# Attention scores of both maps in one double PSUM bank: one maximum for two, the output copy on ScalarE, two factor steps on GpSimd

## The chip, the core and the metric

The kernel runs on one core of one Trainium2 chip. The metric is device time in microseconds (us) of one execution. Of the engines, PE is the matrix engine (its weight loads are listed apart, as PEld), DVE is VectorE, ACT is ScalarE, POOL is GpSimd and SP issues transfers. Every engine works through its own list of instructions in order, and waits where an operand isn't ready.

## What is computed

One inference step of a decoder trunk of two layers, for a prompt of 2048 positions and 8 samples. The change lies in one part of the even layer, the differential attention of the prompt:

```python
def diff_core(q, k, v, allowed, lam):
    s = jnp.einsum('bqhcd,bkhcd->bhcqk', q, k).astype(jnp.float32) * (DIFF_DH ** -0.5)
    p = jax.nn.softmax(jnp.where(allowed, s, -jnp.inf), axis=-1)
    attn = p[:, :, 0] - lam * p[:, :, 1]
    return jnp.einsum('bhqk,bkhd->bqhd', attn.astype(v.dtype), v)
```

Each of 6 heads has two score maps (c = 0 and 1) of 64 channels each. Each map has its own softmax over the keys up to the query's position, and the values (128 wide) are weighted with the first map minus lam times the second. A block of 128 queries sees one to sixteen blocks of 128 keys. What follows per query is an RMS norm of the output.

## The kernel before

The program runs in stages: `in_even` (the input projection, up to about 788 us), `attention` (about 788 to 1395 us), `out_even` (to about 1700 us) and `odd` (the second layer). Only `attention` and the functions it calls are changed.

`attention` (L726) walks over 6 heads and in each over 16 query blocks i of 128 rows, ascending, in the last head descending. `attn_tile` (L789) does one query block. Its keys come in chunks of 512 (`nch` of them, 1 to 4; the last one is 128, 256, 384 or 512 wide).

- Per chunk and map, PE makes the scores `sc` with two matmuls, over the high and the low half of the split keys (L808, L809), and on the last chunk adds the causal mask with a third (L811). DVE takes the negated row maximum `nb` (L812), and ACT the exponential into `p` with the row sum in `l` (L813; the sum is read out by an instruction of its own, READ_ACCUMULATOR).
- When all chunks of the block have their maxima, the factor steps follow (L822 to L832): `m`, the maximum over the chunks (DVE, L824); `f = m - nb` (DVE, L825); exp of it (ACT, L826); `l*f` (DVE, L828), its sum `r` (L829), the reciprocal (L830), times -lam for the second map (L831), and `f*r` (L832), which leaves the factors in `cf`. Blocks with one chunk have two short steps instead (L819, L820).
- Per chunk, POOL multiplies the second map by its factor (L836); in three turns of four DVE then multiplies the first map and adds (L839, one instruction with two inputs), in the fourth POOL does that with two instructions (L841, L842). PE transposes the result, 128 columns at a time (L846, into `tr`), ACT copies it out of PSUM (L848), and PE multiplies it with the values into `pv` (L850).
- At the end of a block DVE copies `pv` to `ob` (L851), and ACT takes the sum of squares of the same `pv` (L853). After four blocks ACT and POOL normalise (L772, L773), PE transposes (`ot`, L783) and ACT scales (L785).

There are 240 chunks (168 of them 512 wide, 24 each of 384, 256 and 128), so 480 score tiles, and 96 blocks, 72 of them with two chunks or more.

PSUM has eight banks of 512 numbers per partition. `bank` (L79) hands them out by kind in turn, and `AT` names them for this stage: four single banks for `sc` ("XXDA", where X has two buffers), two for `tr`, one each for `pv` and `ot`. A bank is given to the next score tile when the exponential over the old one is done. The pool of banks is opened once for the whole program. There are 9 buffers for `p` (`PB`).

The order of the instructions on each engine is set when the program is built: by the order in which the code asks for them and by when the building program takes their inputs to be ready. Work of different chunks and blocks is so interleaved on each engine.

Of the kernel before, what the change touches and what calls it, by code (L numbers as in the profile page):

```python
# [10 lines left out]
F32 = mybir.dt.float32  # L11
# [9 lines left out]
P = 128  # L21
# [24 lines left out]
SP = 0  # L46
AT = dict(sc="XXDA", tr="Y", pv="B", ot="C")
W1, W2, WA, WB, WC = "P", "D", "P", "PD", "PD"
# [13 lines left out]
class Net:  # L62
    def __init__(self, tc, I, O, stop=99):
        self.tc, self.nc, self.I, self.O, self.stop = tc, tc.nc, I, O, stop
        self.root = ExitStack()
        self.const = self.pool(self.root, "const", 1)
        self.sides, self.pace, self.nturn = {}, PC, 0
        self.dram = self.pool(self.root, "dram", 1, DRAM)
        self.ps, self.nbank = self.pool(self.root, "ps", 1, PSUM), {}

    def pool(self, st, name, bufs, space=None, side=None):
# [3 lines left out]
        if side is not None:  # L75
            kw["side"] = side
        return st.enter_context(self.tc.tile_pool(name=name, bufs=bufs, **kw))

    def bank(self, kind, *shape):  # L79
# [617 lines left out]
    def lam_const(self):  # L697
# [13 lines left out]
        nc.vector.scalar_tensor_tensor(self.nlam, e[:, 1:2], -LAM0, e[:, 0:1], ALU.add, ALU.subtract)  # L711
        tmp.close()
        self.sub_w = c.tile([P, 1], F32, name="subw")
        nc.sync.dma_start(self.sub_w, I["subln_w"].rearrange("a d -> d a"), allow_slow_non_contiguous=True)
# [11 lines left out]
    def attention(self):  # L726
        st = ExitStack()
        nc, I = self.nc, self.I
        self.banks = AT


# [43 lines left out]
        self.attn_out(*done, sm)  # L775
        st.close()

    def attn_out(self, h, quad, ob, sm):
# [10 lines left out]
    def attn_tile(self, i, kvt, qt, o, oss, pp, tp, sm):  # L789
# [8 lines left out]
        with self.tc.high_priority(SP) if SP else nullcontext():  # L798
            for j in range(nch):
                n = min(512, nk * P - 512 * j)  # L800
                w = max(n, 256)
                kh, kl = kvt[j][:2]
                p = pp.tile([P, 2, 512], F32, tag="p", name="p")
                for c in range(2):
                    sc = self.bank("sc", 512)
                    qc = qt[:, c, q0:q0 + P]
                    last = j == nch - 1
                    mm(sc[:, :w], qc, kh[:, c, :w], start=True, stop=False)  # L808
                    mm(sc[:, :w], qc, kl[:, c, :w], start=False, stop=not last)  # L809
                    if last:  # L810
                        mm(sc[:, n - P:n], self.identb, self.maskb, start=False, stop=True)  # L811
                    nc.vector.tensor_reduce(nb[:, c, j:j + 1], sc[:, :n], AX.X, ALU.max, negate=True)  # L812
                    nc.scalar.activation(p[:, c, :n], sc[:, :n], AF.Exp, bias=nb[:, c, j:j + 1],  # L813
                                         accum_out=l[:, c, j:j + 1])
# [6 lines left out]
        else:  # L821
            r = sm.tile([P, 2], F32, tag="r", name="r")  # L822
            m = sm.tile([P, 2], F32, tag="m", name="m")
            nc.vector.tensor_reduce(m, nb[:, :, :nch], AX.X, ALU.min)  # L824
            nc.vector.tensor_tensor(f, m[:, :, None].broadcast_to([P, 2, nch]), nb[:, :, :nch], ALU.subtract)  # L825
            nc.scalar.activation(f, f, AF.Exp)  # L826
            lf = l[:, :, :nch]
            nc.vector.tensor_tensor(lf, lf, f, ALU.mult)  # L828
            nc.vector.tensor_reduce(r, lf, AX.X, ALU.add)  # L829
            nc.vector.reciprocal(r, r)  # L830
            nc.vector.tensor_scalar(r[:, 1:2], r[:, 1:2], self.nlam, None, ALU.mult)  # L831
            nc.vector.tensor_tensor(f, f, r[:, :, None].broadcast_to([P, 2, nch]), ALU.mult)  # L832
        pv = self.bank("pv", P)
        for j in range(nch):
# [14 lines left out]
            for t in range(nt):  # L849
                mm(pv, tt[:, t, :], kvt[j][2][:, t, :], start=j == 0 and t == 0, stop=j * 4 + t == nk - 1)  # L850
        nc.vector.tensor_copy(o, pv)  # L851
        junk = sm.tile([P, P], F32, tag="junk", name="junk", bufs=2)
# [800 lines left out]
    def run(self):  # L1653
# [10 lines left out]
        if self.stop > 3:  # L1664
            self.odd()
        self.oddst.close()
        self.root.close()

# [91 lines left out]
```

## Time and profile before

| | us |
|---|---|
| median of 3 runs | 3147.14 (3144.58 to 3152.71) |
| profiled execution, its own time | 3144.06 |
| span of that execution, first to last instruction | 3142.4 |

| stage, window | length | PE busy | PEld | DVE | ACT | POOL |
|---|---|---|---|---|---|---|
| input projection, 0 to 785 | 785 | 725.8 | 707.2 | 421.8 | 366.0 | 415.3 |
| attention, 785 to 1397 | 612 | 549.3 | 454.2 | 557.9 | 476.2 | 422.9 |
| output, 1397 to 1700 | 303 | 265.6 | 233.3 | 206.0 | 80.4 | 181.9 |
| second layer, 1700 to the end | 1443 | 1271.7 | 1121.2 | 984.4 | 593.7 | 668.3 |

Busy time is the union of an engine's instructions. Those of one engine overlap a little at their ends, and PE's a good deal: its matmuls are pipelined, so the distance from one start to the next is shorter than the duration shown. A row of a group gives busy time, mean duration, then the engine's idle time just before these instructions and what ended most of it.

### The profile page before, as it was taken

The numbers are of one execution on the slowest core, as the hardware profiler recorded it, in microseconds if no ns is written. First come the engines' busy times: TensorE is split into PE (matmuls) and PEld (weight loads), VectorE is DVE, ScalarE is ACT, GpSimd is POOL, SyncE is SP. The second block draws the span as 40 slices with busy tenths as digits, with TensorE's granted clock in tenths as the row PEclk, the third lists the DMA queues.
The fourth block names the chain that finished last, engine by engine and source line by source line (L and its number), as shares of the span: only waits on it lengthen the run. The fifth ranks groups of instructions, "written<-read, shape, count | busy, mean of one in ns | idle before, by whom it ended". The sixth has DMA issues, their size and how long they took to land. (4 is left out here: it accounts for less than half of the span.)

```text
span 3142.4 us, 57680 instructions
## 1 busy us (share of the span) xinstructions
PE 2812.4 (89%) x20425; PEld 2515.9 (80%) x20425; DVE 2170.1 (69%) x4012; ACT 1516.3 (48%) x4464; POOL 1688.4 (54%) x1220
## 2 busy tenths in 40 slices
PE   8999899989998899989888778999899988878999
PEld 7999799889777777778777667888788877767887
DVE  5465456464998899876669998658788575457562
ACT  6643245534877787752222223445554533344331
POOL 4566545571667776664665655455544244255541
PEclk9999899999999999999998889999999999979999
DMA  4567766556244423237765554435333233467543
GB/s 164 167 192 254 240 219 202 190 166 183 70 102 118 121 60 84 71 101 221 245 217 180 164 164 160 130 103 154 86 95 100 82 99 112 121 159 212 164 119 98
DMA packets 423149, 462.55 MB, mean 147 GB/s; under 512 B 84683, under 2 KB 324212, under 8 KB 422860
## 3 DMA queue, kind: packets, MB, share of 16 engines
q1 hardware_dynamic: 422860, 458.86, 49.5%
q8 instruction: 162, 2.65, 0.4%
q14 instruction: 127, 1.04, 0.1%
HBM read 332.41 MB, written 126.33 MB: 146 GB/s over the span
## 5 line engine op out<-in xcount | busy, mean ns | idle before, releaser
L184 PE MATMUL acc<-sh,whi 128*128 128x256 f32 (+2 forms) x1328 | 392.5, 296 | 7.4 <-ACT raw L1211 4.8
L186 PE MATMUL acc<-sh,wlo 128*128 128x256 f32 (+2 forms) x1328 | 389.6, 294 | 1.5 <-DVE wlo L165 1.2
L185 PE MATMUL acc<-sl,whi 128*128 128x256 f32 (+2 forms) x1328 | 389.6, 293 | 0.0
L184 PE MATMUL acc<-bh,whi 128*128 128x512 f32 (+2 forms) x904 | 347.4, 384 | 23.9 <-ACT raw L1211 11.2
L186 PE MATMUL acc<-bh,wlo 128*128 128x512 f32 (+2 forms) x904 | 348.5, 386 | 6.6 <-DVE wlo L165 4.1
L185 PE MATMUL acc<-bl,whi 128*128 128x512 f32 (+2 forms) x904 | 346.3, 383 | 1.9 <-DVE bl L873 1.9
L813 ACT ACTIVATE p<-sc,nb 128x512 f32<-128x512 f32 (+3 forms) x480 | 302.3, 642 | 74.0 <-DVE nb L812 63.1
L836 POOL TENSOR_TENSOR p<-p,cf 128x512 f32<-128x512 f32 (+3 forms) x240 | 236.8, 1005 | 182.4 <-DVE cf L832 46.0
L626 POOL TENSOR_TENSOR kp<-kp,at 128x768 f32<-128x768 f32 x120 | 210.9, 1766 | 171.1 <-DMA kp<-in_cache_v 151.9
L165 POOL TENSOR_TENSOR wlo<-wraw,whi 128x1024 fp32r<-128x1024 f32 (+1 forms) x90 | 221.3, 2463 | 127.4 <-ACT whi L163 127.2
L812 DVE TENSOR_REDUCE nb<-sc 128x1 f32<-128x512 f32 (+3 forms) x480 | 276.0, 598 | 17.5 <-PE sc L809 9.1
L184 PEld LDWEIGHTS acc<-sh,whi 128*128 128x128 f32 (+1 forms) x1328 | 260.3, 196 | 17.5 <-ACT raw L1211 6.0
L548 POOL TENSOR_TENSOR kp<-kp,qb 128x768 f32<-128x768 f32 x88 | 168.9, 1925 | 183.6 <-DMA kp<-in_cache_k 133.8
L185 PEld LDWEIGHTS acc<-sl,whi 128*128 128x128 f32 (+1 forms) x1328 | 260.5, 196 | 6.5 <-issue 2.8
L186 PEld LDWEIGHTS acc<-sh,wlo 128*128 128x128 f32 (+1 forms) x1328 | 259.9, 196 | 4.7 <-issue 1.5
L184 PE MATMUL acc<-whi,bh 128*128 128x256 f32 x864 | 249.6, 289 | 0.3 <-DVE th L416 0.3
L185 PE MATMUL acc<-wlo,bh 128*128 128x256 f32 x864 | 248.3, 288 | 0.5 <-POOL wlo L165 0.5
L186 PE MATMUL acc<-whi,bl 128*128 128x256 f32 x864 | 248.4, 288 | 0.0
L1227 DVE SCALAR_TENSOR_TENSOR cx<-raw,convw,cx 128x512 f32<-128x512 f32 x216 | 230.9, 1069 | 11.2 <-ACT cx L1225 8.7
L850 PE MATMUL pv<-v,pt 128*128 128x128 f32 x1632 | 218.7, 282 | 15.9 <-ACT pt L848 9.1
L808 PE MATMUL sc<-kh,q 128*128 128x512 f32 (+2 forms) x480 | 210.5, 439 | 24.4 <-ACT p L813 20.9
L850 PEld LDWEIGHTS pv<-v,pt 128*128 128x128 f32 x1632 | 202.2, 195 | 30.5 <-ACT junk L853 13.8
(443 smaller groups left out, 8344.6 us busy)
## 6 DMA issues: line engine op xcount, KB each, us to landing
kp<-in_cache_k SPq DMA_DIRECT2D x128, 384.0 KB
kp<-in_cache_v SPq DMA_DIRECT2D x128, 384.0 KB
wraw<-in_w_in_e SPq DMA_DIRECT2D x56, 512.0 KB
wraw<-in_w_in_o SPq DMA_DIRECT2D x56, 512.0 KB
mc<-cat SPq DMA_DIRECT2D x72, 256.0 KB
mg<-sg SPq DMA_DIRECT2D x72, 256.0 KB
y<-cth SPq DMA_DIRECT2D x72, 256.0 KB
kh<-kh SPq DMA_DIRECT2D x48, 256.0 KB
```

Of the source, the lines that this page charges most:

```text
L165: e.tensor_tensor(lo, raw, hi.bitcast(F32), ALU.subtract)
L184: mm(out, ah, bh, start=first, stop=False)
L185: mm(out, ah, bl, start=False, stop=False)
L186: mm(out, al, bh, start=False, stop=last)
L548: (nc.vector if j % 3 == 2 else nc.gpsimd).tensor_tensor(k, k, qb, ALU.mult)
L626: nc.gpsimd.tensor_tensor(h3(w), h3(v), self.at[:, b, j, :, None].broadcast_to([P, NH, P]), ALU.mult)
L808: mm(sc[:, :w], qc, kh[:, c, :w], start=True, stop=False)
L812: nc.vector.tensor_reduce(nb[:, c, j:j + 1], sc[:, :n], AX.X, ALU.max, negate=True)
L813: nc.scalar.activation(p[:, c, :n], sc[:, :n], AF.Exp, bias=nb[:, c, j:j + 1], accum_out=l[:, c, j:j + 1])
L836: nc.gpsimd.tensor_tensor(p[:, 1, :n], p[:, 1, :n], cf[:, 1, j:j + 1].broadcast_to([P, n]), ALU.mult)
L850: mm(pv, tt[:, t, :], kvt[j][2][:, t, :], start=j == 0 and t == 0, stop=j * 4 + t == nk - 1)
L1227: nc.vector.scalar_tensor_tensor(x, raw[:, o + j:o + j + 512], w[:, j:j + 1], x, ALU.mult, ALU.add)
```

## The change

Five things change, all in the attention stage.

1. **Double banks.** The scores of both maps of a chunk go into one tile `sc` of two banks, `[P, 2, 512]`, and there are two such tiles (tag "S"). The four banks are the same in number; what is handed out and given back is now a pair. Since the pool of banks is laid out otherwise, it is closed and opened anew before and after the stage (`new_banks`).
2. **One maximum.** After all matmuls of both maps one DVE instruction takes the maxima of both (`nb[:, :, j]`), and then ACT does both exponentials.
3. **`f = m - nb` on POOL** instead of DVE.
4. **The factor -lam.** The step on `r` (L831, DVE) goes away; instead `f` is multiplied by a constant pair `nl2` = (1, -lam) on POOL, after `l*f` has read it and before `f*r`.
5. **The output copy** `o <- pv` on ACT instead of DVE, just ahead of ACT's sum of squares.

```diff
-AT = dict(sc="XXDA", tr="Y", pv="B", ot="C")
+AT = dict(tr="Y", pv="B", ot="C")
...
+    def new_banks(self):
+
+        self.psst.close()
+        self.psst = ExitStack()
+        self.ps = self.pool(self.psst, "ps", 1, PSUM)
...
+        self.nl2 = c.tile([P, 2], F32, name="nl2")
+        nc.gpsimd.memset(self.nl2, 1.0)
+        nc.vector.tensor_copy(self.nl2[:, 1:2], self.nlam)
...
                 p = pp.tile([P, 2, 512], F32, tag="p", name="p")
+                sc = self.ps.tile([P, 2, 512], F32, tag="S", name="sc", bufs=2)
+                last = j == nch - 1
                 for c in range(2):
-                    sc = self.bank("sc", 512)
                     qc = qt[:, c, q0:q0 + P]
-                    last = j == nch - 1
-                    mm(sc[:, :w], qc, kh[:, c, :w], start=True, stop=False)
-                    mm(sc[:, :w], qc, kl[:, c, :w], start=False, stop=not last)
+                    mm(sc[:, c, :w], qc, kh[:, c, :w], start=True, stop=False)
+                    mm(sc[:, c, :w], qc, kl[:, c, :w], start=False, stop=not last)
                     if last:
-                        mm(sc[:, n - P:n], self.identb, self.maskb, start=False, stop=True)
-                    nc.vector.tensor_reduce(nb[:, c, j:j + 1], sc[:, :n], AX.X, ALU.max, negate=True)
-                    nc.scalar.activation(p[:, c, :n], sc[:, :n], AF.Exp, bias=nb[:, c, j:j + 1],
+                        mm(sc[:, c, n - P:n], self.identb, self.maskb, start=False, stop=True)
+
+                nc.vector.tensor_reduce(nb[:, :, j], sc[:, :, :n], AX.X, ALU.max, negate=True)
+                for c in range(2):
+                    nc.scalar.activation(p[:, c, :n], sc[:, c, :n], AF.Exp, bias=nb[:, c, j:j + 1],
                                          accum_out=l[:, c, j:j + 1])
...
-            nc.vector.tensor_tensor(f, m[:, :, None].broadcast_to([P, 2, nch]), nb[:, :, :nch], ALU.subtract)
+            nc.gpsimd.tensor_tensor(f, m[:, :, None].broadcast_to([P, 2, nch]), nb[:, :, :nch], ALU.subtract)
             nc.scalar.activation(f, f, AF.Exp)
             lf = l[:, :, :nch]
             nc.vector.tensor_tensor(lf, lf, f, ALU.mult)
+            nc.gpsimd.tensor_tensor(f, f, self.nl2[:, :, None].broadcast_to([P, 2, nch]), ALU.mult)
             nc.vector.tensor_reduce(r, lf, AX.X, ALU.add)
             nc.vector.reciprocal(r, r)
-            nc.vector.tensor_scalar(r[:, 1:2], r[:, 1:2], self.nlam, None, ALU.mult)
             nc.vector.tensor_tensor(f, f, r[:, :, None].broadcast_to([P, 2, nch]), ALU.mult)
...
-        nc.vector.tensor_copy(o, pv)
+        nc.scalar.copy(o, pv)
```

The instructions stand in a new order on each engine. `attention` calls `self.new_banks()` after `self.banks = AT` and again at its end. In the changed kernel the lines of `attn_tile` have other numbers: L821, L822 and L824 are the score matmuls and the mask, L826 the maximum, L828 the exponential, L839 to L847 the factor steps (L840 and L844 the two on POOL), L851, L854, L856 and L857 the weighting, L861 the transposes, L865 the product with the values, L866 the output copy and L868 the sum of squares.

The numbers in the names tell buffers and tiles apart. PE, third head, the scores of its tenth block (chunks of 512, 512 and 256 columns); `tr` and `pv` belong to earlier blocks. Before:

```order
L808 MATMUL sc_13460<-kh_12850,q_12883 128x512
L809 MATMUL sc_13460<-kl_12851,q_12883 128x512
L808 MATMUL sc_13465<-kh_12850,q_12883 128x512
L809 MATMUL sc_13465<-kl_12851,q_12883 128x512
L846 MATMUL tr_13266<-ident_63,p_13226 128x128 x3
L850 MATMUL pv_13008<-v_12852,pt_13016 128x128 x3
L808 MATMUL sc_13471<-kh_12863,q_12883 128x512
L809 MATMUL sc_13471<-kl_12864,q_12883 128x512
L808 MATMUL sc_13476<-kh_12863,q_12883 128x512
L809 MATMUL sc_13476<-kl_12864,q_12883 128x512
L808 MATMUL sc_13482<-kh_12876,q_12883 128x256
L809 MATMUL sc_13482<-kl_12877,q_12883 128x256
```

And now:

```order
L821 MATMUL sc_13277<-kh_12697,q_12730 128x512
L822 MATMUL sc_13277<-kl_12698,q_12730 128x512
L821 MATMUL sc_13277<-kh_12697,q_12730 128x512
L822 MATMUL sc_13277<-kl_12698,q_12730 128x512
L821 MATMUL sc_13286<-kh_12710,q_12730 128x512
L822 MATMUL sc_13286<-kl_12711,q_12730 128x512
L821 MATMUL sc_13286<-kh_12710,q_12730 128x512
L822 MATMUL sc_13286<-kl_12711,q_12730 128x512
L865 MATMUL pv_13077<-v_12699,pt_13085 128x128 x4
L865 MATMUL pv_13077<-v_12712,pt_13097 128x128 x3
L821 MATMUL sc_13295<-kh_12723,q_12730 128x256
L822 MATMUL sc_13295<-kl_12724,q_12730 128x256
```

Four matmuls, two of each map, now stand together for every chunk; two chunks fill all four banks, and the third chunk's first matmul has to find a pair given back.

DVE at the same block (`nb` maxima, `p` the weighting of earlier chunks, the rest factor steps of earlier blocks). Before:

```order
L831 TENSOR_SCALAR r_13309<-r_13309,nlam_351 128x1
L824 TENSOR_REDUCE m_13398<-nb_13359 128x2
L812 TENSOR_REDUCE nb_13457<-sc_13460 128x1
L832 TENSOR_TENSOR cf_13308<-cf_13308,r_13309 128x2x2
L825 TENSOR_TENSOR cf_13396<-m_13398,nb_13359 128x2x3
L812 TENSOR_REDUCE nb_13457<-sc_13465 128x1
L851 COPY ob_12913<-pv_13008 128x128
L828 TENSOR_TENSOR l_13360<-l_13360,cf_13396 128x2x3
L812 TENSOR_REDUCE nb_13457<-sc_13471 128x1
L829 TENSOR_REDUCE r_13397<-l_13360 128x2
L812 TENSOR_REDUCE nb_13457<-sc_13476 128x1
L812 TENSOR_REDUCE nb_13457<-sc_13482 128x1
```

And now:

```order
L839 TENSOR_REDUCE m_13215<-nb_13182 128x2
L854 SCALAR_TENSOR_TENSOR p_13120<-p_13120,cf_13131 128x512
L826 TENSOR_REDUCE nb_13274<-sc_13277 128x2
L843 TENSOR_TENSOR l_13183<-l_13183,cf_13213 128x2x3
L845 TENSOR_REDUCE r_13214<-l_13183 128x2
L826 TENSOR_REDUCE nb_13274<-sc_13286 128x2
L846 RECIPROCAL r_13214<-r_13214 128x2
L826 TENSOR_REDUCE nb_13274<-sc_13295 128x2
L847 TENSOR_TENSOR cf_13213<-cf_13213,r_13214 128x2x3
L839 TENSOR_REDUCE m_13307<-nb_13274 128x2
L854 SCALAR_TENSOR_TENSOR p_13184<-p_13184,cf_13213 128x512
L826 TENSOR_REDUCE nb_13359<-sc_13362 128x2
```

Two maxima have become one, and L831, L825 and the copy from `pv` are gone from DVE.

POOL, third head, the fourteenth and fifteenth block (four chunks each; the `wo...` row splits a weight of the next stage, `ob` normalises). Before:

```order
L836 TENSOR_TENSOR p_13859<-p_13859,cf_13905 128x512
L836 TENSOR_TENSOR p_13870<-p_13870,cf_13905 128x512
L836 TENSOR_TENSOR p_13881<-p_13881,cf_13905 128x512
L841 TENSOR_TENSOR p_13881<-p_13881,cf_13905 128x512
L836 TENSOR_TENSOR p_13892<-p_13892,cf_13905 128x256
L873 TENSOR_TENSOR wo512l_12905<-wr_13209,wo512h_12904 128x512
L842 TENSOR_TENSOR p_13881<-p_13881 128x512
L773 TENSOR_TENSOR ob_13358<-ob_13358,ss_13357 128x512
L836 TENSOR_TENSOR p_13971<-p_13971,cf_14017 128x512
L836 TENSOR_TENSOR p_13982<-p_13982,cf_14017 128x512
L836 TENSOR_TENSOR p_13993<-p_13993,cf_14017 128x512
L841 TENSOR_TENSOR p_13993<-p_13993,cf_14017 128x512
```

And now:

```order
L840 TENSOR_TENSOR cf_13688<-m_13690,nb_13648 128x8
L888 TENSOR_TENSOR wo512l_12752<-wr_13105,wo512h_12751 128x512
L857 TENSOR_TENSOR p_13558<-p_13558 128x512
L785 TENSOR_TENSOR ob_13181<-ob_13181,ss_13180 128x512
L844 TENSOR_TENSOR cf_13688<-cf_13688,nl2_354 128x8
L851 TENSOR_TENSOR p_13650<-p_13650,cf_13688 128x512
L851 TENSOR_TENSOR p_13659<-p_13659,cf_13688 128x512
L851 TENSOR_TENSOR p_13668<-p_13668,cf_13688 128x512
L856 TENSOR_TENSOR p_13668<-p_13668,cf_13688 128x512
L851 TENSOR_TENSOR p_13677<-p_13677,cf_13688 128x256
L888 TENSOR_TENSOR wo768l_12754<-wr_13176,wo768h_12753 128x512
L840 TENSOR_TENSOR cf_13792<-m_13794,nb_13752 128x8
```

The two new steps of a block (L840, L844) stand behind the weighting of the block before it and ahead of its own, with one to three other instructions between them; in the listing of before no factor step stands on POOL at all.

Ahead of the stage no engine's order is changed but for the setting up of `nl2`. Behind it PE's order is the same row for row until late in the second layer, where single rows change places.

## Rows read from the trace of the kernel before

**Rows 1.** Windows: attention, then 100 us in it; from:to, length, engines busy, clock, DMA.

```profile
785.00:1397.00 612.00, 549.34 (x3724) 454.23 (x3723) 557.86 (x1311) 476.17 (x1554) 422.88 (x397) 0.99 0.33 86
880.00:980.00 100.00, 92.62 (x641) 76.32 (x638) 96.63 (x229) 78.66 (x261) 70.27 (x69) 1.00 0.37 98
```

**Rows 2.** Waits from 790 to 1390: who for whom, us in total, times, longest.

```profile
ACT p L813 <- DVE nb L812: 63.1, 74, 2.8
POOL p L836 <- DVE cf L832: 46.0, 26, 5.7
PEld sc L808 <- ACT p L813: 45.1, 85, 4.3
...
ACT junk L853 <- DVE ob L851: 22.2, 23, 2.8
PE sc L808 <- ACT p L813: 20.9, 39, 4.0
```

**Rows 3.** Groups by form in 785 to 1397, DVE: count, busy us, mean ns, idle before.

```profile
L812 DVE TENSOR_REDUCE nb<-sc 128x1 f32<-128x512 f32 x336 | 222.1, 678 | 11.5 <-PE sc L809 9.1 <-PE sc L811 1.7
L839 DVE SCALAR_TENSOR_TENSOR p<-p,cf 128x512 f32<-128x512 f32 x119 | 138.4, 1166 | 5.1 <-POOL p L836 4.6
...
L851 DVE COPY ob<-pv 128x128 f32<-128x128 f32 x96 | 26.8, 279 | 9.5 <-PE pv L850 9.4
...
L831 DVE TENSOR_SCALAR r<-r,nlam 128x1 f32<-128x1 f32 x72 | 14.8, 206 | 0.7
L812 DVE TENSOR_REDUCE nb<-sc 128x1 f32<-128x128 f32 x48 | 12.6, 277 | 4.3 <-PE sc L811 4.3
```

**Rows 4.** Timeline of DVE, 900 to 903.5: start, duration, instruction.

```profile
899.91 1.26 DVE L812 TENSOR_REDUCE nb<-sc 128x1 f32<-128x512 f32 x2
901.09 0.15 DVE L825 TENSOR_TENSOR cf<-m,nb 128x4 f32<-128x4 f32 x1
...
902.62 0.28 DVE L851 COPY ob<-pv 128x128 f32<-128x128 f32 x1
902.82 0.42 DVE L825 TENSOR_TENSOR cf<-m,nb 128x4 f32<-128x4 f32 x1
```

**Rows 5.** Timeline of POOL around the same time.

```profile
902.18 1.04 POOL L836 TENSOR_TENSOR p<-p,cf 128x512 f32<-128x512 f32 x1 [3.27 <-PE pv L850]
```

**Rows 6.** Line L825: durations min/median/max in ns; then its group (count, busy, mean).

```profile
L825 DVE TENSOR_TENSOR cf<-m,nb x72: 139/168/1059, 798.6 to 1370.2; 128x4 f32<-128x4 f32 x24, 128x6 f32<-128x6 f32 x24, 128x8 f32<-128x8 f32 x24
L825 DVE TENSOR_TENSOR cf<-m,nb 128x4 f32<-128x4 f32 (+2 forms) x72 | 29.2, 406 | 0.6
```

**Rows 7.** Groups by form, ACT and POOL (the last one from the whole program).

```profile
L848 ACT COPY pt<-tr 128x128 f32<-128x128 f32 x24 | 6.8, 281 | 0.0
L836 POOL TENSOR_TENSOR p<-p,cf 128x512 f32<-128x512 f32 x168 | 188.9, 1141 | 136.4 <-DVE cf L832 46.0 <-PE tr L846 17.8 <-PE sc L809 15.0
L890 POOL TENSOR_TENSOR mc<-mc,mg 128x32 f32<-128x32 f32 x2 | 0.5, 254 | 3.4 <-DMA mg<-sg 3.4
```

**Rows 8.** Timeline of PE: scores back to back, products with values, and transposes.

```profile
908.35 0.40 PE L808 MATMUL sc<-kh,q 128*128 128x512 f32 x1
908.58 0.40 PE L809 MATMUL sc<-kl,q 128*128 128x512 f32 x1
908.81 1.05 PE L850 MATMUL pv<-v,pt 128*128 128x128 f32 x8
1387.56 0.60 PE L846 MATMUL tr<-ident,p 128*128 128x128 f32 x4
```

**Rows 9.** Timeline of ACT: two exponentials and their sums read out; PE's next scores.

```profile
903.19 0.77 ACT L813 ACTIVATE p<-sc,nb 128x512 f32<-128x512 f32 x1
...
903.85 0.77 ACT L813 ACTIVATE p<-sc,nb 128x512 f32<-128x512 f32 x1
...
904.42 0.29 ACT L813 ACTIVATION_READ_ACCUMULATOR p<-sc,nb 128x1 f32 x1
904.76 0.19 PEld L808 LDWEIGHTS sc<-kh,q 128*128 128x128 f32 x1 [0.37 <-ACT p L813]
```

**Rows 10.** Tile sc: first and last start of the score matmuls, after count and durations.

```profile
L808 PE MATMUL sc<-kh,q x480: 274/473/775, 787.8 to 1375.9; 128*128 128x512 f32 x115, 128*128 128x256 f32 x29, 128*128 128x384 f32 x16
```

More of the change, by code (lines that the diff above doesn't have):

```diff
@@ L68, in __init__ @@
         self.dram = self.pool(self.root, "dram", 1, DRAM)
-        self.ps, self.nbank = self.pool(self.root, "ps", 1, PSUM), {}
+        self.psst, self.nbank = ExitStack(), {}
+        self.ps = self.pool(self.psst, "ps", 1, PSUM)
     def pool(self, st, name, bufs, space=None, side=None):
@@ L77, in pool @@
         return st.enter_context(self.tc.tile_pool(name=name, bufs=bufs, **kw))
+    def new_banks(self):
+        self.psst.close()
+        self.psst = ExitStack()
+        self.ps = self.pool(self.psst, "ps", 1, PSUM)
     def bank(self, kind, *shape):
@@ L729, in attention @@
         self.banks = AT
+        self.new_banks()
         kv = self.pool(st, "kv", 5)
@@ L776, in attention @@
         st.close()
+        self.new_banks()
     def attn_out(self, h, quad, ob, sm):
@@ L1666, in run @@
         self.oddst.close()
+        self.psst.close()
         self.root.close()
```

## Prediction

> **What bounds the kernel now.** The change touches the attention stage alone, so I read that stage first. The windows by stage [rows 1] show which engine is full: in its 612 us DVE is busy 557.9 (91%, and 97% in the 100 us shown), PE 549, ACT 476, POOL 423. PE's figure flatters it, since its rows overlap: scores of 512 columns start 0.23 us apart and last 0.40; eight products with the values take 1.05 (0.11 apart), four transposes 0.60 (0.11 apart) [rows 8]. By distance between starts PE needs 672 x 0.235 = 158 for the wide scores, 40 for the 288 narrower ones in proportion to their columns, 15 to 45 for the 192 masks (between those distances and their durations), 816 x 0.11 = 90 for transposes, 1632 x 0.11 = 180 for products and 10 for the output's transposes: about 500 us, 82%. DVE is thus the fullest engine, by 9 points.
>
> Who waits for it? The waits [rows 2] name DVE's maxima (ACT, 63.1 us), its last factor step (POOL, 46.0) and its output copy (ACT, 22.2). They name one other thing: PE waits for an exponential to give a score bank back (45.1 us seen by its weight loads, 20.9 by its matmuls, which are the same waits seen twice in part). So the stage has two limits side by side: DVE's work, and the round trip of a score bank, PE to DVE to ACT and back. The change eases the first and tightens the second.
>
> **The change part by part.**
>
> *One maximum for two (DVE, less).* The wide form takes 678 ns, the 128-column one 277 [rows 3]: 1.044 ns a column and 143 ns fixed. One maximum over 2 x 512 is then 143 + 1069 = 1.21 us. Two apart cost 1.36, but two back to back only 1.26 [rows 4], since the start of one hides in the end of the other. DVE is crowded, so I take the latter: 240 x 0.05 = 12 us saved; the bounds are nothing and 240 x 0.143 = 34. [...]
>
> *Steps that leave DVE.* L825: 72, 29.2 us [rows 6]. L831: 72 x 0.206 = 14.8. L851: 96 x 0.279 = 26.8 [rows 3]. Together 71, by distance between starts rather 55 (L851 occupies 0.20 of its 0.28 [rows 4]). DVE goes from 558 to between 475 and 491, 79%.
>
> L825 needs a word. Its median is 168 ns and its maximum 1059 [rows 6]. The row of 0.42 us ends at 903.24, just when POOL's instruction from 902.18 ends, at 903.22 [rows 4, 5]; with POOL idle the same shape took 0.15. So this small step mostly waited for POOL to finish. [...]
>
> *On ACT, more.* 96 copies at 281 ns [rows 7]: 27 us, to about 500 (82%). Against it the wait for DVE's copy goes, 22.2 us [rows 2]; ACT then waits for PE's last product itself, some 9 us by the idle time before L851 [rows 3]. About even.
>
> *On POOL, more.* 144 small steps. The nearest row is 254 ns for 32 columns [rows 7]: 37 us. The bounds are 144 x 0.15 = 22, DVE's price without a wait, and 144 x (0.25 + 0.58) = 120, if each first waits out half a DVE weighting of 1.17 us [rows 3]. POOL goes to about 460 of 612, 75%.
>
> *Closing and opening the banks.* The first pairs wait for the last gate of the stage before, the first banks of the next stage for the last blocks: 0 to 4 us at each end, I take 0, as single banks had to wait for the same users. Behind the stage the order stays, but for single rows late in the second layer: 0, with 5 us to either side.
>
> *The double bank: the round trip.* Price of one trip of a wide chunk, both maps, from rows: four matmuls 3 x 0.235 + 0.40 = 1.10 [rows 8]; maximum 1.21; exponentials 0.66 from the first's start to the second's, 0.86 more until the second's sum is read out at 904.71 [rows 9]; 0.2 for hand-overs (PE's next weight load began 0.05 behind such a read-out [rows 9]; three of them, one longer). Sum 4.0 us. The 72 narrow chunks count 2.8 in the mean by the same sum. All 240: 168 x 4.03 + 72 x 2.8 = 878 us of trips. Score matmuls start from 787.8 to 1375.9 [rows 10], so the banks circulate for some 592 us. With two pairs that leaves 2 x 592 - 878 = 306 us, **1.28 us of waiting per trip**, before the stage gets longer. Before, a single bank's trip was 0.63 + 0.68 + 0.86 + 0.2 = 2.4, about 2.07 in the mean over the forms, and four banks left 4 x 592 - 480 x 2.07 = 1374 us, 2.9 per trip. So the slack falls to less than half, and what decides is how long a trip has to wait.
>
> A floor: when a trip arrives, DVE is in work of its own two fifths of the time, ACT a third, PE half, with about 0.5, 0.3 and 0.35 us of it left: 0.2 + 0.1 + 0.2 = 0.5. The ceiling is the 2.9 of before, much of which was queueing for the fullest engine, which is less full now. Since each engine keeps a fixed order, a trip also waits where its turn isn't next: behind two weightings on DVE (2 x 1.17), or behind copies on ACT. I take 1.15, with 0.8 to 1.65 as the likely span: the stage changes by 120 x (1.15 - 1.28) = **-15 us** (-58 to +44).
>
> **The sum.** DVE's 65 to 85 us less are not on the path once DVE stands at 80%: PE, ACT and the banks are next, all within 3 points. What reaches the end is the round trip's -15; ACT +0, ends 0, second layer 0. From the profiled execution's 3144.06 us: 3129. The median of the runs shown is 3.1 us above that execution; 3130 serves for both.
>
> **The rivals.**
>
> *The banks bind (slower).* If a trip waits 1.6 us, the stage takes 120 x 0.32 = 38 us more: about 3183. It decides from 1.28 us on. For it: PE already waits for exponentials with four banks [rows 2]; and in the new order the third chunk's scores stand behind two chunks that fill all banks. Against it: 2.9 us of before included DVE's queue at 97%.
>
> *POOL's factor steps bind (slower).* The first (L840) stands behind the whole weighting of the block before, and the second (L844) can't start until ACT has made the exponential and DVE `l*f`; nothing behind it on POOL moves meanwhile, and ACT stands at the exponential. POOL has 612 - 460 - 20 (both ends) = 132 us idle, 1.8 per block with factor steps. The chain: 0.25 for POOL's own step, about 0.25 for a small exponential, 0.3 and 0.5 for what runs on ACT and DVE just then, 0.15 for `l*f`, another 0.5 on DVE, 0.3 of hand-overs: 2.2, less about 0.7 of other work between the two steps: 1.5. At 2.3 it costs 72 x 0.5 = 36 us: 3180. [...]
>
> *DVE's relief comes through in full (faster).* Then PE bounds the stage, at the 92% that DVE reaches now: 500 / 0.92 = 543, 65 us less: 3080. For it: ACT's and POOL's longest waits name DVE [rows 2]. Against it: the slack of the trips would have to be 0.75 us.
>
> *No change.* The steps leave DVE, but it only idles more, and the trips wait their 1.28: 3144.
>
> **How the numbers follow.** A measurement of this kernel can tell some 0.3% (9.4 us) from no change. Modest gain, 10 to 45 us less: 0.34. Full relief: 0.07. No change within 9.4 us: 0.24. Banks bind: 0.21. POOL's chain binds: 0.14. So faster 0.41, same 0.24, slower 0.35. The likeliest case is the modest gain, 3130, with a range of its own from 3099 to 3134. Gains and losses both hold much of the chance, so the range reaches across: 3096 leaves out most of the full relief, 3185 the worse half of the two slow rivals, together two in ten.
>
> **What would show it.** DVE's busy time in the stage at 475 to 491 us; the 240 wide maxima of 2 x 512 at 1.21 us each (more than 1.36 would make that part a loss); ACT's wait for the output copy gone; PE's wait for exponentials risen from 45 us to some 80 to 120. If it is above 150 and the stage is longer than 612 us, the banks bind. If instead POOL's idle time before L844 and L851, and ACT's before the small exponential (L841), grew together to over 130 us, POOL's chain does. If the stage is near 545 us, PE's rows would stand nearly without gaps and I have overrated the trips. A change of over 10 us outside 785 to 1397 would show that the reopened banks or the new order late in the second layer matter.

## The result, and the profile after

The changed kernel took 3183.07 us, the median of four runs (3181.43 to 3190.52), beside 3146.17 for the kernel before: a ratio of 1.0118 (95% interval 1.01 to 1.0136), slower by some 37 us. The profiled execution took 3190.52 us, with a span of 3188.8.

The loss is in the attention stage first. Two rows give its length, from the first score matmul to the last output copy; they are groups by tile, with count, min/median/max duration in ns, first and last start. After the change:

```profile
L821 PE MATMUL sc<-kh,q x480: 274/398/776, 784.7 to 1399.8; 128*128 128x512 f32 x115, 128*128 128x256 f32 x29, 128*128 128x384 f32 x16
...
L866 ACT COPY ob<-pv x96: 248/267/470, 794.0 to 1416.6; 128x128 f32<-128x128 f32 x96
```

From 784.7 to 1416.6 that is 631.9 us. Before it was 607.6, from 787.8 [rows 10] to the last output copy's start, 1395.4:

```profile
L851 DVE COPY ob<-pv x96: 265/278/292, 796.3 to 1395.4; 128x128 f32<-128x128 f32 x96
```

So the stage became 24.3 us longer. The window of the stage (columns as in [rows 1]):

```profile
782.00:1418.00 636.00, 550.04 (x3717) 461.82 (x3715) 493.31 (x830) 494.37 (x1649) 453.95 (x539) 0.98 0.31 80
```

DVE's 557.9 us became 493.3, as planned, and it is now busy 78% of the stage instead of 91%. No engine takes its place: ACT also stands at 78%, PE at 86%. What grew is waiting. The waits in that window (who for whom, us in total, times, longest), to be held against [rows 2]:

```profile
ACT p L828 <- DVE nb L826: 62.8, 80, 2.5
PEld sc L821 <- ACT p L828: 59.0, 72, 3.1
POOL cf L844 <- DVE l L843: 58.3, 46, 2.8
POOL p L851 <- DVE cf L847: 44.3, 45, 2.6
DVE nb L826 <- PE sc L822: 44.2, 51, 2.5
PE sc L821 <- ACT p L828: 41.1, 58, 2.8
...
ACT pt L863 <- PE tr L861: 28.9, 32, 4.2
DVE nb L826 <- PE sc L824: 27.0, 33, 3.9
...
ACT ob L866 <- PE pv L865: 12.1, 19, 2.2
```

DVE, which had hardly a gap, now waits 71 us for scores (44.2 + 27.0; 16.5 before). ACT waits 28.9 us for transposes, where that wait was 6.3 before:

```profile
ACT pt L848 <- PE tr L846: 6.3, 8, 2.3
```

PE's wait for score banks went from 45.1 and 20.9 to 59.0 and 41.1. ACT's wait for the maxima stayed at 63.

How these waits hang together can be seen in 6 us of the timeline (start, duration, instruction, and in brackets the idle time before it with its releaser):

```profile
999.88 1.28 POOL L857 TENSOR_TENSOR p<-p 128x512 f32<-128x512 f32 x1
...
1000.40 1.82 DVE L826 TENSOR_REDUCE nb<-sc 128x2 f32<-128x1024 f32 x2 [1.10 <-PE sc L822]
...
1001.22 1.09 PE L861 MATMUL tr<-ident,p 128*128 128x128 f32 x8 [0.18 <-POOL p L857]
...
1001.91 0.59 ACT L863 COPY pt<-tr 128x512 f32<-128x512 f32 x1 [2.09 <-PE tr L861]
...
1002.39 0.69 ACT L828 ACTIVATE p<-sc,nb 128x512 f32<-128x512 f32 x1
...
1003.16 0.69 ACT L828 ACTIVATE p<-sc,nb 128x512 f32<-128x512 f32 x1
...
1003.73 0.21 ACT L828 ACTIVATION_READ_ACCUMULATOR p<-sc,nb 128x1 f32 x1
...
1003.99 0.50 PE L821 MATMUL sc<-kh,q 128*128 128x512 f32 x1 [0.17 <-ACT p L828]
...
1004.79 0.39 PE L822 MATMUL sc<-kl,q 128*128 128x512 f32 x1
...
1005.22 1.23 DVE L826 TENSOR_REDUCE nb<-sc 128x2 f32<-128x1024 f32 x1 [0.73 <-PE sc L822]
```

The joint maximum that begins at 1000.40 is over after some 1.2 us, at 1001.6. ACT has nothing to do, but the next instruction in its order is a copy of earlier transposes, which wait for POOL's weighting. For most of the 2.09 us that ACT idles there is no finished maximum either; from 1001.6 on there is one, and its first exponential still stands behind the copy until 1002.39. The copy holds it up by some 0.8 us, 0.3 of idling and 0.5 of copying. The two exponentials follow, the second's sum is read out at 1003.94, and 0.05 us later PE starts the next scores in that pair of banks. DVE then has to wait for all four matmuls. So in this place a bank's trip does not lead through PE, DVE and ACT alone: by ACT's fixed order it also leads through POOL's weighting and PE's transposes.

The groups by form (count, busy us, mean ns, idle before) give the prices of the new instructions:

```profile
L826 DVE TENSOR_REDUCE nb<-sc 128x2 f32<-128x1024 f32 x168 | 204.0, 1218 | 50.3 <-PE sc L822 44.2 <-PE sc L824 5.5 <-PE tr L861 0.2
...
L866 ACT COPY ob<-pv 128x128 f32<-128x128 f32 x96 | 27.4, 286 | 12.3 <-PE pv L865 12.1
...
L840 POOL TENSOR_TENSOR cf<-m,nb 128x8 f32<-128x8 f32 x24 | 7.3, 303 | 5.1 <-DVE m L839 5.1
...
L844 POOL TENSOR_TENSOR cf<-cf,nl 128x8 f32<-128x8 f32 x24 | 4.9, 206 | 25.1 <-DVE l L843 24.7
```

Some 12 us of the 37 lie outside the stage (22 of 46 in the profiled execution, the slowest of the four). The other 17 kernels of this study in which the stage can be marked in the same way show that this part moves without new banks too: the median time minus the stage of the profiled execution is between 2530 and 2551 us for all of them (before 2539, after 2551). Most of the spread is in the second half of the second layer. There, from about 2640 us on in the trace of before, the traces show two orders of the instructions on DVE, ACT and POOL. But for a few rows, eight kernels have the order of before (2530 to 2544 us, 2537 in the mean), nine that of after (2534 to 2551, 2544 in the mean), and the kernel with the steps alone, below, has one of its own (2536). So some 7 us go with that order, on average. It does not need the new banks: a kernel whose only edit is the output copy has it too. The granted clock differs as well; here are three windows at about the same place, of before, of after, and of that kernel:

```profile
2873.00:2979.00 106.00, 102.33 (x899) 92.61 (x899) 67.98 (x163) 43.77 (x164) 62.99 (x52) 1.00 0.64 177
```

```profile
2913.00:3022.00 109.00, 98.23 (x828) 88.32 (x825) 67.27 (x156) 42.98 (x160) 61.06 (x50) 0.95 0.56 158
```

```profile
2878.00:2988.00 110.00, 94.51 (x764) 84.88 (x762) 65.99 (x153) 38.55 (x144) 57.10 (x49) 0.94 0.53 152
```

The clock (third column from the end, as a share of its highest) was 1.00 in the first window, and 0.95 and 0.94 in the other two; in the window of after the trace shows 0.50 for 10.2 of the 109 us. The windows do not hold quite the same work; counted back from the end of the program, the 897 matmuls that start in the first of them take 106, 114 and 121 us. Whether the other order brings the lower clock is not shown. Executions of one kernel differ too: ten of the kernel before took 3139 to 3155 us, at a mean clock of 0.953 to 0.960. Below, the length of the stage in the profiled execution therefore stands beside each time. It is one execution each; two with the same code in the stage (the kernel before, and the one with its banks reopened) differ by 3.6 us.

### The profile page after: what moved, and what is told of

It reads as the page before. It is cut to its first block, busy times and chain, and to the rows that moved or that the text cites. A ratio compares the mean times of both kernels' runs of the same rounds, so it can differ in the third digit from the quotient of the medians.

```text
span 3188.8 us, 57413 instructions
## 1 busy us (share of the span) xinstructions
PE 2825.7 (89%) x20425; PEld 2534.4 (79%) x20425; DVE 2106.7 (66%) x3533; ACT 1536.8 (48%) x4560; POOL 1728.9 (54%) x1365
## 3 DMA queue, kind: packets, MB, share of 16 engines
q14 instruction: 123, 1.01, 0.1%
## 5 line engine op out<-in xcount | busy, mean ns | idle before, releaser
L828 ACT ACTIVATE p<-sc,nb 128x512 f32<-128x512 f32 (+3 forms) x480 | 299.7, 638 | 68.6 <-DVE nb L826 62.8
L826 DVE TENSOR_REDUCE nb<-sc 128x2 f32<-128x1024 f32 (+3 forms) x240 | 252.9, 1059 | 72.4 <-PE sc L822 44.2
L851 POOL TENSOR_TENSOR p<-p,cf 128x512 f32<-128x512 f32 (+3 forms) x240 | 236.3, 1003 | 108.8 <-DVE cf L847 44.3
L821 PE MATMUL sc<-kh,q 128*128 128x512 f32 (+2 forms) x480 | 205.8, 429 | 43.0 <-ACT p L828 41.1
L865 PE MATMUL pv<-v,pt 128*128 128x128 f32 x1632 | 222.2, 282 | 9.8 <-ACT pt L863 7.6
L865 PEld LDWEIGHTS pv<-v,pt 128*128 128x128 f32 x1632 | 207.1, 195 | 21.8 <-ACT pt L863 11.7
```

What stands on the lines that cost most here:

```text
L821: mm(sc[:, c, :w], qc, kh[:, c, :w], start=True, stop=False)
L826: nc.vector.tensor_reduce(nb[:, :, j], sc[:, :, :n], AX.X, ALU.max, negate=True)
L828: nc.scalar.activation(p[:, c, :n], sc[:, c, :n], AF.Exp, bias=nb[:, c, j:j + 1], accum_out=l[:, c, j:j + 1])
L851: nc.gpsimd.tensor_tensor(p[:, 1, :n], p[:, 1, :n], cf[:, 1, j:j + 1].broadcast_to([P, n]), ALU.mult)
```

## The experiments

**The two halves of the change.** The first kernel has the double banks, the joint maximum and the reopened banks, the second the rest.

```diff
 # banks alone, against the changed kernel
-            nc.gpsimd.tensor_tensor(f, m[...], nb[...], ALU.subtract)
+            nc.vector.tensor_tensor(f, m[...], nb[...], ALU.subtract)
...
-            nc.gpsimd.tensor_tensor(f, f, self.nl2[...], ALU.mult)
...
+            nc.vector.tensor_scalar(r[:, 1:2], r[:, 1:2], self.nlam, None, ALU.mult)
...
-        nc.scalar.copy(o, pv)
+        nc.vector.tensor_copy(o, pv)
```

> The change's bank part alone: double score banks, one maximum for two, banks closed and opened anew; all factor steps and the output copy are on DVE as before. Theory B (the two double banks bind: a pair's round trip leaves too little slack): the loss is already here, 3165 to 3190 us, PE waiting 90 us or more for exponentials (66 before). Theory P (the two factor steps on POOL hold up POOL and all behind it): no loss without them, 3125 to 3150, PE's wait near 66.

> The other half of the change: the two factor steps on POOL and the output copy on ACT, but four single score banks and one maximum per map, as before. Theory B: no loss, 3115 to 3150, since DVE is relieved of 71 us and the banks are as loose as before. Theory P: the loss is here, 3165 to 3190, with POOL's idle time before its second factor step (L844 in the changed kernel, 62 us there) still 50 us or more.

Measured: the banks alone 3189.93 us (ratio 1.0138, 1.0107 to 1.017), the steps alone 3127.26 (0.994, 0.991 to 0.9969). The stage in the two, by the same two rows each:

```profile
L821 PE MATMUL sc<-kh,q x480: 274/398/797, 784.4 to 1412.5; 128*128 128x512 f32 x115, 128*128 128x256 f32 x29, 128*128 128x384 f32 x16
...
L866 DVE COPY ob<-pv x96: 264/277/293, 794.4 to 1427.6; 128x128 f32<-128x128 f32 x96
```

```profile
L819 PE MATMUL sc<-kh,q x480: 274/473/774, 784.6 to 1358.5; 128*128 128x512 f32 x115, 128*128 128x256 f32 x29, 128*128 128x384 f32 x16
...
L862 ACT COPY ob<-pv x96: 253/278/576, 792.7 to 1376.1; 128x128 f32<-128x128 f32 x96
```

643.2 and 591.4 us (from the unrounded starts), against 607.6. Theory P falls and theory B stands in its sign: the whole loss is in the bank part, and the steps alone are a kernel faster than both, though POOL waits there too for its second factor step (40.0 us).

**Single steps taken back.** The changed kernel with its factor steps on DVE, and with its output copy on DVE.

> The whole change, but the two factor steps and the factor -lam are on DVE as before. Theory B: the loss stays, 3170 to 3195 (DVE has some 44 us more than in the changed kernel). Theory P: the loss goes, 3125 to 3150.

> The whole change, but the output copy is on DVE as before. Theories B and P: both about the time of the changed kernel, 3170 to 3195. A third theory, A (ACT, which now makes the copy and stands idle until PE's last product is done, holds back the exponentials behind it and so the banks): 3135 to 3155.

Measured: 3169.48 us (stage 633.9) and 3183.13 (643.5). Without POOL's factor steps the stage is as long as with them (631.9), so they are not what holds it up. The whole time fell by 14 us, all of it outside the stage, where this kernel has the order of before. Theory P's and theory A's times were both missed, and theory B's for the first kernel by half a us. The copy on ACT is worth 12 us of stage (643.5 to 631.9) and nothing of the whole time (3183.13 and 3183.07): the kernel with the copy on DVE has the order of before outside the stage, too.

**The reopened banks.**

```diff
 # against the kernel before; new_banks itself, and nl2, as in the change
         self.banks = AT
+        self.new_banks()
...
         st.close()
+        self.new_banks()
```

> The kernel before with the pool of banks closed and opened anew ahead of the attention stage and behind it, and nothing else. The four kernels with double banks took 7 to 15 us more behind the attention stage than the kernel before or the one with the steps alone (1758 to 1772 against 1747 and 1751 in the profiled executions). Theory R (the reopened banks cost that): 3152 to 3162, the attention stage as before. Theory N (it has another cause, the length of the stage before it or chance): 3140 to 3151.

Measured: 3151.3 us, ratio 1.003 (1.0016 to 1.0044), between the two theories' ranges. The stage took 611.2 us, 3.6 more than before, and the rest of the program what it takes elsewhere (2540). So some 9 us (5 to 14) may belong to the reopening, of which the profile shows 4 in the stage; late in the second layer this kernel has the order of after, which other kernels have without reopened banks.

**The joint maximum.** Double banks alone with two maxima, in two code orders: one maximum behind each map's scores, and both behind all scores.

```diff
-                nc.vector.tensor_reduce(nb[:, :, j], sc[:, :, :n], AX.X, ALU.max, negate=True)
                 for c in range(2):
+                    nc.vector.tensor_reduce(nb[:, c, j:j + 1], sc[:, c, :n], AX.X, ALU.max, negate=True)
+                for c in range(2):
                     nc.scalar.activation(p[:, c, :n], sc[:, c, :n], AF.Exp, bias=nb[:, c, j:j + 1],
```

> Double score banks alone, but with one maximum for each map, right behind that map's scores, as before; factor steps and output copy as before. What is left of the change is that two banks are handed out and given back together. Theory B1 (handing them out as pairs is the cost): as in the run of the bank part alone (3190), 3170 to 3200. Theory B2 (the joint maximum is the cost, since the first map's exponential now waits for the second map's scores and for 1.21 us of maximum where it took 0.68): 3140 to 3160.

> Double score banks alone with the scores of both maps together as in the changed kernel, but two maxima, each over its own half, and then the two exponentials. It differs from the run of the bank part alone (3190) in the joint maximum only. In the earlier run with two maxima the second map's scores waited for the first map's exponential, because both lie in one tile; here they stand ahead of both maxima. Theory B1 (handing two banks out and back together is the cost): 3185 to 3210, the joint maximum being a small gain. Theory B2 (the joint maximum is the cost): 3140 to 3170.

Measured: 3270.15 us (stage 733.3) with a maximum behind each map, 3181.97 (stage 642.3) with both behind all scores. The second is the clean comparison: beside 643.2 with the joint maximum, the joint maximum costs and gains nothing in the stage. Its time lies between the two theories' ranges, 3 us below that of B1. The first had another fault: its two maps share a tile, and in its order on PE the second map's scores stand behind other chunks and wait for the first map's exponential, so that a pair serves as one bank at a time. PE waited 136.2 us (weight loads) and 79.2 us (matmuls) for exponentials there, 81.8 and 56.3 in the second.

**Single steps on the kernel before.** The output copy on ACT alone, and the factor steps on POOL alone.

> The kernel before with the output copy on ACT, nothing else. With double banks that move was worth 20 us (3190 without it, 3169 with it). Theory C (ACT no longer waits 22 us for DVE's copy, and DVE is relieved of 27): 3118 to 3135, so the 20 us of the run with the steps alone are the copy's. Theory F (they come from the factor steps): 3141 to 3152.

> The kernel before with the two factor steps on POOL and the factor -lam there, nothing else. Theory C (the gain of the steps is the copy's): 3141 to 3158. Theory F (relief of DVE by 44 us gains it): 3122 to 3137.

Measured: 3145.48 us (1.0007, 0.9991 to 1.0024; stage 602.4) and 3151.79 (1.003, 1.0009 to 1.0051; stage 601.6). Neither alone gains time, and both together gain 0.6%. In the stage they are worth 5, 6 and 16 us; what the factor steps lose in the whole time lies outside the stage (2550), where both kernels have the order of after. Theory C had the time of the second right and theory F that of the first, so neither half explains the gain of both.

**Fewer single banks.** The kernel before, with three and with two of its four.

```diff
-AT = dict(sc="XXDA", tr="Y", pv="B", ot="C")
+AT = dict(sc="XXD", tr="Y", pv="B", ot="C")
```

> The kernel before with three single score banks in place of four; one bank stays empty, nothing else is changed. In the trace of before a bank is held for 4.13 us in the mean, from its first score matmul to the read-out of its exponential's sum; 480 of these in 594 us are 3.3 banks in use. Theory B (score banks are near their limit, the kernel can't spare a part of them): 20 to 80 us more, 3165 to 3225. Theory O (banks are not what the double-bank kernel lacks): within 10 us, 3137 to 3157.

> The kernel before with two single score banks in place of four. By the prices of the prediction, a trip of a single bank takes 2.07 us in the mean; 480 of them leave 2 x 592 - 994 = 190 us to wait, 16% of the two banks' time. Four singles leave 58%, three 44% (10 us longer than before), two double banks 26% (35 to 45 us longer with the rest as before). Theory B (this share decides): more than the double banks, 3200 to 3300. Theory O: 3150 to 3185.

Measured: 3152.71 us (1.0037, 1.0022 to 1.0051; stage 622.1) and 3260.58 (1.0377, 1.035 to 1.0405; stage 731.0). In the stage four, three and two banks take 607.6, 622.1 and 731.0; two pairs, at 642, lie between three singles and two. The time does rise with the scarcity of banks, in the order of the shares of free time that the expectation gives. Two singles came out as theory B had it, but three as theory O had it, within 10 us of the kernel before. And the wait of PE for banks alone does not set the price, as the waits of three singles and of the double banks alone show:

```profile
PEld sc L808 <- ACT p L813: 80.6, 137, 2.1
PE sc L808 <- ACT p L813: 41.1, 81, 2.0
...
ACT pt L848 <- PE tr L846: 8.6, 10, 1.8
```

```profile
PEld sc L821 <- ACT p L828: 80.6, 91, 3.5
...
PE sc L821 <- ACT p L828: 55.3, 72, 3.0
...
ACT pt L863 <- PE tr L861: 25.9, 26, 2.0
```

PE's weight loads waited 80.6 us for banks in both, but the stage is 21 us longer with pairs. Among what differs is ACT's wait for transposes, 8.6 and 25.9 us (6.3 before, 9.5 with the steps alone); DVE's waits for scores (23.5 and 41.6 us) and that of PE's matmuls grew as well.

**A third pair.** Six banks for scores leave two of the eight that the kernel lays out, so something else must give. In the first two kernels the transposes and the norm's transposes share a single bank. In the other three the product with the values goes into its chunk's transposes' bank (`mm(pt[:, 0, :], ...)`), which leaves the transposes two. These three leave out the adding up of the chunks' products, so they tell of time alone.

> The whole change with three double banks in place of two; for that the transposes and the norm's transposes share one bank (three banks before). To be read against its twin with two double banks. Theory B (the round trip of the pairs binds): a third pair gives each trip 2.5 us more to wait, so 25 to 60 us less than the twin. Theory O (the new order on the engines costs the time, whatever the number of banks): within 10 us of the twin.

> The whole change with two double banks, and with the transposes and the norm's transposes in one bank, as in the kernel with three pairs: its twin. It tells what that one bank costs by itself: both theories expect 3185 to 3225, above the changed kernel.

> The whole change with three double score banks and two banks for the transposes. To have the room, the product with the values goes into the bank of its own chunk's transposes once they are copied, and the norm's transposes use the same two banks; so the chunks' products aren't added up and the output is that of each block's last chunk. Each engine's work is the same. Read against its two twins: theory B (two double banks are too few trips' worth): at least 25 us below the twin with two pairs, and within 20 of the twin with four singles. Theory O (pairs cost the time by their order on the engines, whatever their number): within 10 us of the twin with two pairs.

> Twin with two double score banks, the products again in the transposes' banks and not added up. Both theories: 30 to 70 us above the twin with four singles, if this layout keeps the effect that is to be explained (56 us between the changed kernel, 3183, and the run with the steps alone, 3127). Within 10 us of it, the layout would hide the effect and the three runs would tell nothing.

> Twin with four single score banks and one maximum per map, the products again in the transposes' banks and not added up: the factor steps on POOL and the output copy on ACT as in the change. 3110 to 3150 by both theories, near the run with the steps alone.

Measured: three and two pairs 3202.03 and 3208.48 us in the first layout (stage 660.6 and 662.4); three pairs, two pairs and four singles 3177.95, 3171.7 and 3161.42 in the second (632.6, 637.5 and 617.1). In the first layout the waits of three pairs, and of two:

```profile
ACT pt L863 <- PE tr L861: 81.5, 119, 5.7
...
PEld sc L821 <- ACT p L828: 21.9, 61, 1.5
```

```profile
ACT pt L863 <- PE tr L861: 69.9, 103, 2.6
PEld sc L821 <- ACT p L828: 57.1, 94, 2.1
```

The third pair takes away most of PE's wait for banks (57.1 to 21.9), and the stage hardly moves: ACT's wait for transposes, long already with the single bank, grows by 12. The second layout hides a good part of the effect (20 us of stage and 10 of the whole time between pairs and singles, where 40 and 56 were to be explained; the four singles lie above the range expected for them), so it decides less than was hoped; in it the third pair gives 5 of the 20 in the stage, and the whole time is 6 us longer. In both layouts the third pair came out as theory O had it, within 10 us of its twin, and not as theory B. By the rows of the 240 chunks with three pairs in that layout, a trip takes 7.3 us, and 3.1 of them lie between the end of the maximum and the start of the first exponential: the added bank waits for ACT's turn. Neither layout is that of the change, and a third pair in that one has no room.

**Taken together, given back singly.** Four single banks and two maxima, but all scores of a chunk as one unbroken group on PE.

> The kernel before, with four single banks and two maxima, but the scores of both maps as one unbroken group on PE that starts when both banks are free, as with the double bank; each bank is given back by itself, when its own exponential is read out. Theory T (taking two banks together and making all scores of a chunk in one go is the cost): 3170 to 3200, like the double banks with two maxima (3182). Theory G (giving the two banks back together is the cost): 3138 to 3157, like the kernel before.

> The run with the steps alone (3127: four single banks, two maxima, factor steps on POOL, output copy on ACT), but the scores of both maps as one unbroken group that starts when both banks are free. The changed kernel differs from it in giving the banks back together and in the joint maximum. Theory T: 3160 to 3190. Theory G: 3118 to 3140.

Measured: 3795.83 and 3800.91 us. Both are far above either theory, since the unbroken group has a price of its own. The waits of the first:

```profile
DVE nb L814 <- PEq L806: 671.5, 237, 11.6
PEld sc L809 <- issue: 460.0, 240, 11.9
```

Ahead of each of the 240 groups PE stood 1.9 us in the mean (460.0 / 240) without waiting for anything that the profile shows. The granted clock was 0.884 in the mean of the profiled execution, and 0.958 before. If the stage alone made the difference, and the 654 us by which the span grew, the two spans and clocks give some 0.75 in the stage (an estimate), where before 0.99 was measured. Four transposes that start at 1000.85 in its timeline took 1.08 us, four before 0.60 [rows 8]. The runs say nothing about the banks.

## Why the prediction was wrong

The forecast was 3130, faster, and the kernel was slower. 3183 is the time that the rival "the banks bind" gave, and lies inside the range of 3096 to 3185, but on the side of the losses. That it is this rival's time to the microsecond is partly chance: its 38 us were all in the stage, and of the 37 measured 24 are.

- **What bounds the kernel.** DVE as the fullest engine and the trip of a bank as the second limit: borne out by the halves. DVE's relief alone shortens the stage by 16 us, the pairs alone lengthen it by 36.
- **The joint maximum.** Forecast 1.21 us a piece; measured 1218 ns (for the 168 wide ones; the prediction speaks of 240 of that size). The maxima took 279.1 us of DVE in 480 instructions and now 253.5 in 240 (both are sums over the forms): 25.6 us less, between the 12 that was taken and the upper bound of 34.
- **Steps that leave DVE.** 475 to 491 us were forecast for DVE's busy time, 493.3 came out, just above.
- **POOL.** 37 us were forecast for 144 small steps; the six groups of L840 and L844 add up to 36.8, far from the bound of 120, the author's estimate for steps that each first wait for a weighting. The rival that they bind falls: with them back on DVE the stage is not shorter (633.9, 631.9 with them). Its sign did not come either: the idle times that were to grow together to over 130 us (before L844, L851 and L841) are 183 us after, and were 194 before, at L836 and L826.
- **ACT.** 27 us more busy time: 27.4. The wait for DVE's copy is gone, 12.1 us for PE's product stand in its place (9 forecast). Not foreseen was the wait for transposes, 28.9.
- **The banks closed and opened anew.** Taken at 0, with 0 to 4 us at each end. The profile shows 3.6 in the stage; the timed runs allow 5 to 14 in all.
- **Outside the stage.** Taken at 0, with 5 us to either side; 12 came (22 in the profiled execution). The sign for this part, more than 10 us outside, did come, and some 7 us go with the new order late in the second layer.
- **The round trip, the step that failed.** The price of a trip without waiting was 3.66 us in the mean, and 1.15 us of waiting was taken for it, below the break-even of 1.28. In the trace after, a trip takes 4.62 us from the first score matmul to the read-out, worked out from the rows of the 240 chunks, and the pair then stands free for 0.50 until the next scores: 1.46 of waiting, near the rival's 1.6. The term that was mis-sized is the waiting, 1.15 taken and 1.46 measured. It stands at 0.58 ahead of DVE, 0.42 ahead of ACT and 0.50 ahead of PE (1.50 in all; the rest of the trip took 3.62, a little less than its price). By the prediction's own formula that is 120 x (1.46 - 1.28) = +22 us; the stage became 24 longer. With the banks alone the trip waits 1.59, so +37, and the stage became 36 longer. The formula is bookkeeping, though: a longer stage shows as longer trips whatever makes it longer.
- **Where in the waiting.** The floor of 0.5, for what an engine has in hand when a trip arrives, was about right: by the rows of the 240 chunks it is 0.60 (0.32 on DVE, 0.13 on ACT, 0.14 on PE, whose ends are modelled). Too small was the 0.65 that was added for turns that are not next: some 0.9 us of a trip's waiting is spent on other instructions that stand ahead of it in an engine's order (0.26 on DVE, 0.29 on ACT, 0.35 on PE). With the banks alone the two parts are 0.60 and 1.06. In nearly all of it the engine is at work; it idles for 0.15 us of a trip's waiting. The place in the timeline above, where ACT idles, is thus not the common case; whether the instructions ahead came late because of idling further back was not measured.
- **The sign that was announced for this case** (PE's wait above 150 us) did not come, nor the 80 to 120 of the forecast: 59.0 for the weight loads, which had 45 before, and 41.1 for the matmuls, partly the same waits. Three singles have more of it and lose less. It was the wrong sign; the wait spread to DVE (71 us for scores) and to ACT.

That the loss comes from handing out score banks in pairs is shown, by the halves and by the kernel with two maxima over double banks. That scarcity of banks is a part of it fits the series of four, three and two singles; that it is all of it does not fit the third pair. Why pairs cost what they cost is therefore not shown. Whether the rest comes from taking two banks together, from giving them back together, or from the order that is built around the pairs stays open: the runs meant to part these carried a cost of their own.

## What to carry to other kernels

Relief of the fullest engine is worth little when it is paid with a coarser hand-over on the loop that feeds it: the steps taken off DVE, some 55 us of its time, gave 16 us of stage with single banks (607.6 to 591.4) and 11 with pairs (643.2 to 631.9), and the pairs had cost 36. Count what a resource waits for by asking what stands ahead of its instruction in each engine's fixed order, not only what the engine has in hand: here 0.9 us of a trip's waiting came from the first and 0.6 from the second. Look outside the part that was changed, too: the order of instructions there can change with it. Where a change has parts that need not go together, time them apart: here half of it, kept alone, is the faster kernel (3127 us, 0.6% below the one before).

## What the runs showed of the hardware that was not expected

- The granted clock late in the second layer was 1.00 in one window of 106 us, and 0.95 and 0.94 at about the same place in two other kernels, whose instructions stand in another order there. The time outside the changed stage ranged over 21 us (2530 to 2551), more than half of the effect that was to be explained.
- An unbroken group of instructions on PE cost 1.9 us of idle time ahead of it in the mean, with a granted clock of 0.884 over the profiled execution (0.958 before), and made the kernel 1.21 times as long (1.2052 to 1.2155).
- Two small gains that are each next to nothing alone (5 and 6 us of the stage, and none in the whole time) were worth 16 us of the stage together. The 5 us above their sum are little more than the 3.6 by which two profiles of the same stage differ.
